# A decoder layer on one core: a later start for the down products' splits and loads, another order in the attention, outputs in steps

## The chip, the cores and the metric

The kernel runs on one NeuronCore of a Trainium2 chip. The metric is the device time of one execution in microseconds; the time given for a kernel is the median of several executions. A profile is taken of one more execution. TensorE does the matrix products and transposes, VectorE, ScalarE and GpSimd (in the profile DVE, ACT and POOL) do the rest, and SyncE (SP) only starts transfers.

## The reference

One layer of a hybrid decoder over 1024 tokens of width 1024, in float32:

```
h = x
h = h + 0.5 * swiglu(rms_norm(h), ffn1_w_gu, ffn1_w_down)
h = h + hybrid_mixer(rms_norm(h), ...)     # sparse attention, 8 heads | gated recurrence, 4 heads
h = h + 0.5 * swiglu(rms_norm(h), ffn2_w_gu, ffn2_w_down)
out = rms_norm(h)

swiglu(x) = (silu(gate) * up) @ w_down,  gate, up = x @ w_gu   # hidden width 2752
```

The attention has three branches for each head, each with its own softmax: over compressed keys (63 of them), over all earlier tokens (with 16 blocks of 64 tokens and 16 of them selected, the selected branch sees every earlier block), and over a window of 512 tokens. Scores carry a linear bias by distance. The three outputs are summed with sigmoid gates.

## The kernel before

**Numbers in two parts.** Every large product is done with operands split into a high part rounded for the fast float32 mode and a low part, the rest. `split` (L174) makes the high part on ScalarE (L180) or GpSimd (L178) and the low part on VectorE (L182). A product is three matmuls: high x high, high x low, low x high (L186 to L188 in `mm3`, L731 to L733 in `down`). The operand that streams through TensorE is read in an interleaved order there: `il` takes elements 0, n/2, 1, n/2+1 and so on, and whoever reads the result takes `ev(b)`, which undoes it.

**The two FFNs.** Both halves of each FFN use Strassen's scheme with seven products for eight. The up products (`up_rest`, `up_strassen`, `up_last`) run over 22 blocks of 128 hidden columns. Their results, and sums of them, go to DRAM as `H[...]` (`hid_put`, L548 to L562). For the last two blocks these stores sit on ScalarE's queue: the very last things that the up products put into the queues of VectorE and ScalarE are a subtraction (L562) and the store of its result (L556). Sums of the down weights are made on the way (`down_sums`, L581).

The second half, `down` (L700), has seven stages n with eleven steps m each. Step (n, m) loads a tile of the hidden sums and one of the down weights (L739 to L747, 256 KB each, on SP's queue), splits both, and adds 12 matmuls to four banks. Loads can run six steps ahead, for there are six pairs of buffers. The split tiles have their own buffers, two steps' worth in a pool that is open during the up products already. After some stages the four banks are added to the residual tiles `h` (`add`, L712), either at once or, from copies, at steps (n+1, 3), (n+1, 5), (n+1, 7) and (n+1, 9), as `later` says. `after` holds further work for given steps: the loads of the eight residual tiles (512 KB each, L1513 and L1811, eight steps from (0, 1) to (1, 4)), and in the first FFN the norm and the first weights of the mixer.

**What sets the order.** The program is written as one sequence. Tile, the layer below, puts the instructions of each engine in an order of its own at compile time, by the sequence and by when it expects operands to be ready, and an engine then takes its queue strictly in that order. So an instruction whose operands come early can be placed far ahead of its place in the program. `issue_after(i)` forbids that: what is traced under it stands behind `i` on the engine of `i`. `late()` (L143) does so for the last instruction traced so far on each of ScalarE, GpSimd, VectorE and SP.

**The attention.** For each of eight blocks of 128 queries (qb) and two groups of four heads (g), `att_soft` (L1216) does one head: score products (`prod`, L1239 and L1240), the bias and the row minimum in one VectorE instruction (`red`, L1245), exponentials with row sums on ScalarE (L1282), the reciprocal of the three sums on VectorE (L1285 for the first two heads together, L1288 for the others), and a scaling by reciprocal and gate on GpSimd (L1294). `att_pv` (L1299) then takes the four heads of a unit together: for each block of keys four transposes into a bank (L1325, two such banks), a copy to a high part on ScalarE (L1327), a low part on VectorE (L1328), and two value products (`pv`, L1316), which run two blocks behind. It is a generator that is advanced between the heads of the next unit.

**The end.** `finish` (L1817) is called for each token tile once per half of its columns. After the second it makes the final norm: a square sum, a power on GpSimd (`rsqrt`, L200), the scaled halves on VectorE (L1835) and ScalarE (L1843), and two stores of 256 KB.

Of the kernel before, what the change touches and what calls it, by code (L numbers as in the profile page):

```python
# [94 lines left out]
class Net:  # L95
# [15 lines left out]
    def consts(self, ctx):  # L111
        tc, nc = self.tc, self.nc
        c = self.cp = ctx.enter_context(tc.tile_pool(name="const", bufs=1))
        it = c.tile([128, D], F32, name="iota", tag="gb")[:, :128]
        nc.gpsimd.iota(it, pattern=[[1, 128]], base=0, channel_multiplier=-1,
                       allow_small_or_imprecise_dtypes=True)
        self.ident = c.tile([128, 128], F32, name="ident")
        self.mhalf = c.tile([128, 16], F32, name="mhalf")
        nc.gpsimd.memset(self.mhalf[:], -0.5)
        nc.vector.tensor_scalar(self.ident[:], it, 0.0, None, op0=OP.is_equal)  # L120

    def load_gain(self, ap):
# [16 lines left out]
        self.turn = 1 - self.turn  # L139
        return self.bank("ba"[self.turn])  # L140

    @contextmanager
    def late(self, pe=False):  # L143

        last = {}
        for i in self.nc.cur_bb.bb.instructions:
            last[i.engine] = i
        E = mybir.EngineType
        with ExitStack() as c:
            for e in (E.Activation, E.Pool, E.DVE, E.SP) + pe * (E.PE,):  # L150
                if e in last:
                    c.enter_context(self.tc.issue_after(last[e]))
            yield
# [547 lines left out]
    def down(self, pool, pool2, name, H, h, scale, final, after=(), wide=None, tail=0):  # L701
# [17 lines left out]
            return [nat(t[:]) for t in out]  # L719

        stages = (("A11", "B11"), ("A12", "B21"), ("S2", "T2"), ("S3", "T3"), ("A22", "T4"), ("S1", "T1"), ("S4", "B22"))
        later, behind = {}, None
        for n, (an, bn) in enumerate(stages):
            if n in (0, 2, 5):
                bs = [self.bank("b" if n == 2 else "a") for _ in range(4)]
# [9 lines left out]
            for m in range(11):  # L735
                i = n * 11 + m
                p, nb = (pool, 8) if i % 6 < 4 else (pool2, 4)
                raw, hr = (p.tile([128, 512], F32, name=self.nm("dr"), tag="dr", bufs=nb) for _ in range(2))
                nc.sync.dma_start(out=hr[:], in_=H[an][m])  # L739
                if bn in H:  # L740
                    nc.sync.dma_start(out=raw[:], in_=H[bn][m])
                else:
                    j, c = 2 * m + (bn != "B11"), 512 * (bn == "B22")
                    k = min(128, FF - j * 128)
                    if k < 128:
                        nc.gpsimd.memset(raw[k:], 0.0)
                    nc.sync.dma_start(out=raw[:k], in_=w_down[j * 128:j * 128 + k, c:c + 512])  # L747
                if wide is None and n < 6 and i % 5 > 1:
                    t2 = [self.xp.tile([128, 2, 512], F32R, name=self.nm("dw"), tag="xT", bufs=16) for _ in range(2)]
                    hh, hl, dh, dl = (t[:, k, :] for t in t2 for k in range(2))  # L750
                else:
                    p, nb = (pool2, 12) if wide and i % 5 > 1 else (pool, 8)
                    hh, hl, dh, dl = (p.tile([128, 512], F32R, name=self.nm("dw"), tag="dw", bufs=nb)[:] for _ in range(4))
                with self.tc.issue_after(behind) if behind and m > 1 else nullcontext():
                    self.split(hh, hl, hr[:], "act")
                self.split(dh, dl, raw[:])
                if n == 6 and m >= 11 - tail:
                    left.append((m, hh, hl, dh, dl))
# [456 lines left out]
    def att_soft(self, p, g, qb, hh):  # L1215
# [18 lines left out]
        wc = (qb + 1 - lo) * 128  # L1234
        cmp = P2[:, wc:wc + 64]

        def prod(ka, kl):
            b = self.bank()[:, :ka.shape[1]]
            mm(b, qa[:, qc], ka, start=True, stop=False)  # L1239
            mm(b, qa[:, qc], kl, start=False, stop=True)  # L1240
            return b

        def red(b, dst, tab, br, j):
            out = st[:, br:br + 1] if j == 0 else st[:, 9 + br:10 + br]
            nc.vector.tensor_tensor_reduce(out=dst, in0=b, in1=tab, op0=OP.add, op1=OP.min, scale=-slope,  # L1245
                                           scalar=3.0e38 if j == 0 else st[:, br:br + 1], accum_out=out)
            return out
# [3 lines left out]
        for br, s in ((2, 1), (1, 0)):  # L1251
            k0 = 0 if s == 0 else lo
            j = 0
            for half in range(2):
# [4 lines left out]
                c = (a % 4) * 128 + (0 if s else 576 - 64 * half)  # L1259
                pre = 64 if s == 0 and half == 0 and qb < 3 else 0  # L1260
                post = 64 if s == 1 and half == 0 and qb > 4 else 0
                b = prod(self.KA[g, half][:, c - pre:c + w + post], self.KL[g, half][:, c - pre:c + w + post])
                if pre:
                    bc = b[:, :64]
                if post:
# [3 lines left out]
                else:  # L1269
                    dst = P2[:, (a - lo) * 128:(e - lo) * 128]  # L1270
                    tab = self.dwin[:, 512 + (a - qb) * 128:512 + (e - qb) * 128]
                m = red(b[:, pre:pre + w], dst, tab, br, j)
                j += 1
            mx.append((br, m))
        if bc is None:
# [4 lines left out]
        def rest():  # L1280
# [1 line left out]
                nc.scalar.activation(out=rng[br], in_=rng[br], func=AF.Exp, scale=-1.0, bias=m,  # L1282
                                     accum_out=st[:, 6 + br:7 + br])
            if hh == 1:
                nc.vector.reciprocal(out=both[:, :, 6:9], in_=both[:, :, 6:9])  # L1285
                scaled(h - 1, both[:, 0, :], *before)
            elif hh:
                nc.vector.reciprocal(out=st[:, 6:9], in_=st[:, 6:9])  # L1288
            if hh:
                scaled(h, st, rng)  # L1290

# [8 lines left out]
    def att_pv(self, p, g, qb, Ps, raw, M):  # L1300
# [18 lines left out]
        for n, (i, c, w, v) in enumerate(blocks):  # L1319
# [8 lines left out]
            nc.vector.tensor_tensor(out=l[:w], in0=b[:w], in1=h[:w].bitcast(F32), op=OP.subtract)  # L1328
            th.append(h)
            tl.append(l)  # L1330
            if n > 1:
                pv(n - 2)
        pv(last - 1)
        pv(last)
        yield
        tmp = p.tile([128, 4, 128], F32, name=self.nm("ot"), tag="ph", bufs=4)[0:64]
        nc.scalar.activation(out=tmp.rearrange("p h (a b) -> p h a b", a=2), in_=ev(O[64:128], 64), func=AF.Copy)
        qc = slice((qb % 4) * 128, (qb % 4) * 128 + 128)
# [26 lines left out]
def body(ctx, tc, ins, out):  # L1365
# [146 lines left out]
        with net.late():  # L1512
            nc.sync.dma_start(out=h[tt][:], in_=x[tt * 128:(tt + 1) * 128, :])  # L1513

    for i, tt in enumerate((4, 5, 6, 7, 0, 1, 2, 3)):
        after[(0, 2 * i + 1) if i < 5 else (1, 2 * i - 10)] = lambda tt=tt: load(tt)

    def final(tt, c):
        net.square(np_, h[tt][:, c * 512:c * 512 + 512], sq[tt // 4][:, c, tt % 4:tt % 4 + 1])
# [283 lines left out]
    np_ = pool(ctx, "n3", "right")  # L1803
    net.load_gain(ins["final_norm"][None, :])
    h = [hp.tile([128, D], F32, name=f"k{tt}") for tt in range(NT)]
    sq = [np_.tile([128, 2], F32, name=f"sk{tt}") for tt in range(NT)]
    after, pend = {}, []

    def reload(tt):
        with net.late():  # L1810
            nc.sync.dma_start(out=h[tt][:], in_=spilled(tt))  # L1811

    for i, tt in enumerate((4, 5, 6, 7, 0, 1, 2, 3)):
        after[(0, 2 * i + 1) if i < 5 else (1, 2 * i - 10)] = lambda tt=tt: reload(tt)

    def finish(tt, c):
        k = slice(c * 512, c * 512 + 512)  # L1817
# [10 lines left out]
        y = np_.tile([128, D], F32, name=net.nm("y"), tag="y", bufs=4)  # L1828

        def store(i):  # L1830
            k = slice(i * 512, i * 512 + 512)
            (nc.sync if 4 <= tt < 7 or tt == 7 and i else nc.scalar).dma_start(out=out[0, tt * 128:(tt + 1) * 128, k], in_=y[:, k])

        def second():
            nc.vector.scalar_tensor_tensor(out=y[:, k], in0=hv, scalar=r, in1=net.gb[:, k], op0=OP.mult, op1=OP.mult)  # L1835
            store(1)

        r = net.rsqrt(np_, sq[tt][:, 0:1], 1, 1, "rs", sq[tt][:, 1:2])
        if 4 <= tt < 7:
# [4 lines left out]
        store(0)  # L1844

    net.down(f2, f2b, "ffn2", H, h, lambda tt: 0.5, finish, after, True, 5)
    cd.close()
# [18 lines left out]
```

## Time and profile before

| | us |
|---|---|
| median of 3 runs | 1904.49 (1901.87 to 1904.88) |
| the profiled execution | 1908.84 |
| its span, first to last instruction | 1907.1 |
| TensorE busy | 1876.7 (98%) |
| VectorE busy | 1348.6 (71%) |
| ScalarE busy | 787.2 (41%) |
| GpSimd busy | 524.4 (27%) |
| start of the down products, first FFN | 422.83 |
| start of the down products, second FFN | 1698.07 |
| last matmul starts | 1899.68 |

A matmul of 128x512 is shown with 0.38 us, but the next starts 0.215 us after it: matmuls are pipelined and their ends are modelled. TensorE's busy share says little; the distance from one start to the next, or the number of matmuls in a stretch, says whether it is held up. In a row of a timeline the first number is the start, the second the duration, and what stands in brackets is the idle time before it and what ended it. In a row of stretches each engine has its busy time and its number of instructions, and then come the granted share of TensorE's clock, the share of the DMA engines and GB/s. In a row of waits stand the sum, the number and the longest.

### The profile page before, as it was taken

How to read it: one execution, taken by the hardware profiler on the slowest of the kernel's cores; microseconds unless marked ns; L12 is line 12 of the kernel's file. 1: busy time of each engine (PE TensorE's matmuls, PEld its weight loads, DVE VectorE, ACT ScalarE, POOL GpSimd, SP SyncE). 2: the span in 40 equal slices, each digit the busy share in tenths (PEclk: the TensorE clock that was granted, in tenths of full speed). 3: DMA queues.
4: the chain of work that ended last, by engine and by line, in shares of the span. 5: the costliest groups of instructions: out<-in, count | busy, mean ns of one | idle time of the engine just before them, and what ended most of it. 6: DMA issues, size and time to landing. Idle time of an engine off the chain costs nothing.

```text
span 1907.1 us, 31154 instructions
## 1 busy us (share of the span) xinstructions
PE 1876.7 (98%) x11054; PEld 1622.4 (85%) x11054; DVE 1348.6 (71%) x2596; ACT 787.2 (41%) x1665; POOL 524.4 (27%) x634
## 2 busy tenths in 40 slices
PE   9999999999999999999999999999999999999998
PEld 6888888888888888889887788888888888888886
DVE  5988778658775545777278888836867777558676
ACT  5533333322323412333389776646333333323233
POOL 2133233324342001111156444311222222123222
PEclk9999999999999999999999999999999999999999
DMA  5346666438675132443321022462456676157664
GB/s 199 103 136 220 226 213 232 138 116 287 220 260 164 70 105 95 140 136 134 133 67 46 15 79 74 151 234 87 157 180 220 217 231 213 63 187 263 210 213 149
DMA packets 161787, 304.30 MB, mean 160 GB/s; under 512 B 17600, under 2 KB 47328, under 8 KB 161632
## 3 DMA queue, kind: packets, MB, share of 16 engines
q1 hardware_dynamic: 152096, 285.79, 45.4%
q10 hardware_dynamic: 9536, 16.53, 2.5%
q8 instruction: 87, 1.43, 0.3%
q14 instruction: 68, 0.56, 0.1%
HBM read 213.65 MB, written 88.60 MB: 158 GB/s over the span
## 4 chain that ended last, share of the span: by engine, by line
PE 84%; DVE 7%; ACT 3%; issue 2%; DMA 1%; POOL 1%; SPq 0%; POOLq 0%; DVEq 0%; ACTq 0%
PE b L186 17%; PE b L187 17%; PE b L188 17%; PE b L733 6%; PE b L731 6%; PE b L732 6%; PE b L1325 3%; PE b L1316 2%; PE b L1240 1%; PE b L1239 1%; ACT P L1282 1%; ACT ph L1327 1%; PE b L925 1%; PE b L796 1%; PE b L797 1%
## 5 line engine op out<-in xcount | busy, mean ns | idle before, releaser
L186 PE MATMUL b<-xT,wp 128*128 128x512 f32 x1196 | 455.4, 381 | 4.4 <-DVE pd L687 4.1
L187 PE MATMUL b<-xT,wp 128*128 128x512 f32 x1196 | 454.5, 380 | 1.5 <-DVE xT L425 1.3
L188 PE MATMUL b<-xT,wp 128*128 128x512 f32 x1196 | 453.8, 380 | 0.0
L182 DVE TENSOR_TENSOR dw<-dr,dw 128x512 fp32r<-128x512 f32 x308 | 231.5, 798 | 68.6 <-ACT dw L180 47.6
L186 PEld LDWEIGHTS b<-xT,wp 128*128 128x128 f32 x1196 | 226.6, 189 | 41.3 <-DVE pd L687 5.3
L187 PEld LDWEIGHTS b<-xT,wp 128*128 128x128 f32 x1196 | 226.5, 189 | 35.2 <-DVE xT L425 3.6
L188 PEld LDWEIGHTS b<-xT,wp 128*128 128x128 f32 x1196 | 226.4, 189 | 32.5
L733 PE MATMUL b<-dw,dw 128*128 128x512 f32 x616 | 235.1, 382 | 2.7 <-DVE dw L182 2.7
L731 PE MATMUL b<-dw,dw 128*128 128x512 f32 x616 | 235.2, 382 | 1.3 <-DVE dw L182 1.3
L732 PE MATMUL b<-dw,dw 128*128 128x512 f32 x616 | 234.5, 381 | 0.0
L178 POOL TENSOR_SCALAR dw<-dr 128x512 fp32r<-128x512 f32 x154 | 127.8, 837 | 254.8 <-PE b L733 130.6
L180 ACT ACTIVATE wp<-ws 128x512 fp32r<-128x512 f32 x148 | 92.9, 629 | 233.3 <-PE b L187 225.5
L180 ACT ACTIVATE dw<-dr 128x512 fp32r<-128x512 f32 x154 | 92.2, 625 | 198.7 <-PE b L731 88.0
L1294 POOL TENSOR_SCALAR P<-P,sm,gate 128x64 f32<-128x64 f32 (+8 forms) x192 | 125.7, 673 | 168.4 <-DVE sm L1285 99.1
L182 DVE TENSOR_TENSOR wp<-ws,wp 128x512 fp32r<-128x512 f32 x148 | 113.4, 768 | 30.7 <-ACT wp L180 30.5
L733 PEld LDWEIGHTS b<-dw,dw 128*128 128x128 f32 x616 | 117.1, 190 | 20.5 <-DVE dw L182 3.8
L731 PEld LDWEIGHTS b<-dw,dw 128*128 128x128 f32 x616 | 117.2, 190 | 18.8 <-issue 1.4
L732 PEld LDWEIGHTS b<-dw,dw 128*128 128x128 f32 x616 | 117.2, 190 | 16.8
L180 ACT ACTIVATE wp<-wr 128x512 fp32r<-128x512 f32 x115 | 71.9, 626 | 142.0 <-PE b L187 119.7
L1282 ACT ACTIVATE P<-P,sm 128x64 f32<-128x64 f32 (+8 forms) x192 | 114.7, 600 | 28.5 <-DVE sm L1245 27.5
L186 PE MATMUL b<-xT,wh 128*128 128x512 f32 x320 | 125.8, 394 | 0.0
L521 POOL TENSOR_TENSOR ws<-wr 128x512 f32<-128x512 f32 x37 | 51.6, 1396 | 263.9 <-DVE wp L182 215.4
(308 smaller groups left out, 3554.9 us busy)
## 6 DMA issues: line engine op xcount, KB each, us to landing
dr<-hs SPq DMA_DIRECT2D x242, 256.0 KB, 4.0
wr<-in_ffn_w_gu_dram SPq DMA_DIRECT2D x82, 512.0 KB, 4.2
hs<-hk SPq DMA_DIRECT2D x140, 256.0 KB, 3.9
hs<-wd SPq DMA_DIRECT2D x88, 256.0 KB, 3.1
wd<-in_ffn_w_down_dram SPq DMA_DIRECT2D x84, 256.0 KB, 3.5
dr<-in_ffn_w_down_dram SPq DMA_DIRECT2D x62, 256.0 KB, 4.2
wq<-wo SPq DMA_DIRECT2D x40, 256.0 KB, 2.9
wo<-wo SPq DMA_DIRECT2D x16, 512.0 KB, 2.6
```

What stands on the lines that cost most here:

```text
L178: nc.gpsimd.tensor_scalar(out=hi, in0=src, scalar1=1.0, scalar2=1.0, op0=OP.mult, op1=OP.mult)
L180: nc.scalar.activation(out=hi, in_=src, func=AF.Copy)
L182: eng.tensor_tensor(out=lo, in0=src, in1=hi.bitcast(F32), op=OP.subtract)
L186: mm(ps, wh, xh, start=first, stop=False, skip_group_check=skip)
L187: mm(ps, wh, xl, start=False, stop=False, skip_group_check=skip)
L188: mm(ps, wl, xh, start=False, stop=last, skip_group_check=skip)
L731: mm(bs[t][:], hl[:, c], dh, start=first, stop=False, skip_group_check=True)
L732: mm(bs[t][:], hh[:, c], dh, start=False, stop=False, skip_group_check=True)
L733: mm(bs[t][:], hh[:, c], dl, start=False, stop=last, skip_group_check=True)
L1282: nc.scalar.activation(out=rng[br], in_=rng[br], func=AF.Exp, scale=-1.0, bias=m, accum_out=st[:, 6 + br:7 + br])
L1294: nc.gpsimd.tensor_scalar(out=rng[br], in0=rng[br], scalar1=st[:, 6 + br:7 + br], scalar2=self.gate[:, qb, h * 3 + br:h * 3 + br + 1], op0 ...
L1325: nc.tensor.transpose(b[:w, hh * 128:hh * 128 + 128], Ps[hh][i][:, c:c + w], self.ident[:])
```

## The change

- `down` of both FFNs: the splits of steps m=1 to 10 of stage 0 stand behind the last instruction that each engine had when `down` was called. Those of m=0 stay free.
- The residual loads move from after steps (0, 1), (0, 3), (0, 5), (0, 7), (0, 9), (1, 0), (1, 2), (1, 4) for tiles 4 to 7 and 0 to 3 to (0, 5), (0, 7), (0, 9), (0, 10), (1, 1), (1, 2), (1, 4), (1, 5) for tiles 4, 0, 5, 1, 6, 2, 7, 3.
- Attention: score products whose bank holds no compressed part (no `pre`, no `post`) read the keys interleaved, and `red` undoes it. The sums are inverted by a power of -1 on GpSimd. Value products are issued in pairs after every second block, and the last two or three after the generator's last stop, so behind the next head's scores.
- The end: tiles 0 to 3 are no longer scaled in `finish`. One power serves all four, and steps (6, 3) to (6, 7) scale and store one tile each, on ScalarE's queue.

```
-        nc.gpsimd.memset(self.mhalf[:], -0.5)
+        nc.gpsimd.memset(self.mhalf[:, :8], -0.5)
+        self.mone = self.mhalf[:, 8:14]
+        nc.gpsimd.memset(self.mhalf[:, 8:], -1.0)
...
-    def late(self, pe=False):
+    def late(self, pe=False, last=None):
+        last = last or self.lasts()
...
-        later, behind = {}, None
+        later, behind, entry = {}, None, self.lasts()
...
-                with self.tc.issue_after(behind) if behind and m > 1 else nullcontext():
-                    self.split(hh, hl, hr[:], "act")
-                self.split(dh, dl, raw[:])
+                with self.late(last=entry) if n == 0 and m else nullcontext():
+                    with self.tc.issue_after(behind) if behind and m > 1 else nullcontext():
+                        self.split(hh, hl, hr[:], "act")
+                    self.split(dh, dl, raw[:])
...
+            if turn:
+                ka, kl = il(ka), il(kl)
             mm(b, qa[:, qc], ka, start=True, stop=False)
...
+            if turn:
+                dst, b, tab = nat(dst), ev(b), nat(tab)
             nc.vector.tensor_tensor_reduce(out=dst, in0=b, in1=tab, op0=OP.add, op1=OP.min, scale=-slope,
...
+                turn = not pre and not post
...
-                nc.vector.reciprocal(out=both[:, :, 6:9], in_=both[:, :, 6:9])
+                nc.gpsimd.tensor_tensor(out=both[:, :, 6:9], in0=both[:, :, 6:9], in1=self.mone.rearrange("p (a b) -> p a b", a=2), op=OP.pow)
...
-                nc.vector.reciprocal(out=st[:, 6:9], in_=st[:, 6:9])
+                nc.gpsimd.tensor_tensor(out=st[:, 6:9], in0=st[:, 6:9], in1=self.mone[:, :3], op=OP.pow)
...
-            if n > 1:
+            if n > 2 and n % 2:
+                pv(n - 3)
                 pv(n - 2)
-        pv(last - 1)
-        pv(last)
         yield
+        for n in range((last - 1) // 2 * 2, last + 1):
+            pv(n)
...
-    for i, tt in enumerate((4, 5, 6, 7, 0, 1, 2, 3)):
-        after[(0, 2 * i + 1) if i < 5 else (1, 2 * i - 10)] = lambda tt=tt: load(tt)
+    for g, tt in zip((5, 7, 9, 10, 12, 13, 15, 16), (4, 0, 5, 1, 6, 2, 7, 3)):
+        after[g // 11, g % 11] = lambda tt=tt: load(tt)
...
+    def early(tt):
+        with net.late():
+            if tt == 0:
+                Z["r"] = net.rsqrt(np_, sq4[:, 0, :], 4, 1, "rs4", sq4[:, 1, :])
+            if tt:
+                store(tt - 1, Z["y"], 1, nc.scalar)
+            if tt < 4:
+                r = Z["r"][:, tt:tt + 1]
+                y = Z["y"] = np_.tile([128, D], F32, name=net.nm("y"), tag="y", bufs=4)
+                nc.vector.scalar_tensor_tensor(out=y[:, 512:], in0=h[tt][:, 512:], scalar=r, in1=net.gb[:, 512:], op0=OP.mult, op1=OP.mult)
+                nc.scalar.activation(out=y[:, :512], in_=h[tt][:, :512], func=AF.Copy, scale=r)
+                store(tt, y, 0, nc.scalar)
+
+    for i in range(5):
+        after[6, 3 + i] = lambda tt=i: early(tt)
```

More of the change, by code (lines that the diff above doesn't have):

```diff
@@ L140, in bank2, with lasts @@
         return self.bank("ba"[self.turn])
-    @contextmanager
-    def late(self, pe=False):
+    def lasts(self):
         last = {}
@@ L147, in late @@
             last[i.engine] = i
+        return last
+    @contextmanager
+    def late(self, pe=False, last=None):
+        last = last or self.lasts()
         E = mybir.EngineType
@@ L1235, in att_soft, with prod @@
         cmp = P2[:, wc:wc + 64]
-        def prod(ka, kl):
+        def prod(ka, kl, turn=False):
             b = self.bank()[:, :ka.shape[1]]
+            if turn:
+                ka, kl = il(ka), il(kl)
             mm(b, qa[:, qc], ka, start=True, stop=False)
@@ L1241, in prod, with red @@
             return b
-        def red(b, dst, tab, br, j):
+        def red(b, dst, tab, br, j, turn=False):
             out = st[:, br:br + 1] if j == 0 else st[:, 9 + br:10 + br]
+            if turn:
+                dst, b, tab = nat(dst), ev(b), nat(tab)
             nc.vector.tensor_tensor_reduce(out=dst, in0=b, in1=tab, op0=OP.add, op1=OP.min, scale=-slope,
@@ L1261, in att_soft @@
                 post = 64 if s == 1 and half == 0 and qb > 4 else 0
-                b = prod(self.KA[g, half][:, c - pre:c + w + post], self.KL[g, half][:, c - pre:c + w + post])
+                turn = not pre and not post
+                b = prod(self.KA[g, half][:, c - pre:c + w + post], self.KL[g, half][:, c - pre:c + w + post], turn)
                 if pre:
@@ L1271, in att_soft @@
                     tab = self.dwin[:, 512 + (a - qb) * 128:512 + (e - qb) * 128]
-                m = red(b[:, pre:pre + w], dst, tab, br, j)
+                m = red(b[:, pre:pre + w], dst, tab, br, j, turn)
                 j += 1
@@ L1805, in body @@
     h = [hp.tile([128, D], F32, name=f"k{tt}") for tt in range(NT)]
-    sq = [np_.tile([128, 2], F32, name=f"sk{tt}") for tt in range(NT)]
-    after, pend = {}, []
+    sq4 = np_.tile([128, 2, 4], F32, name="sk")
+    sq = [sq4[:, :, tt] if tt < 4 else np_.tile([128, 2], F32, name=f"sk{tt}")[:] for tt in range(NT)]
+    after, pend, Z = {}, [], {}
     def reload(tt):
@@ L1811, in reload @@
             nc.sync.dma_start(out=h[tt][:], in_=spilled(tt))
-    for i, tt in enumerate((4, 5, 6, 7, 0, 1, 2, 3)):
-        after[(0, 2 * i + 1) if i < 5 else (1, 2 * i - 10)] = lambda tt=tt: reload(tt)
+    for g, tt in zip((5, 7, 9, 10, 12, 13, 15, 16), (4, 0, 5, 1, 6, 2, 7, 3)):
+        after[g // 11, g % 11] = lambda tt=tt: reload(tt)
     def finish(tt, c):
@@ L1827, in finish @@
             return
[L1828 to L1832, printed above, removed]
+        if tt < 4:
+            return
         def second():
             nc.vector.scalar_tensor_tensor(out=y[:, k], in0=hv, scalar=r, in1=net.gb[:, k], op0=OP.mult, op1=OP.mult)
-            store(1)
+            store(tt, y, 1, nc.sync)
+        y = np_.tile([128, D], F32, name=net.nm("y"), tag="y", bufs=4)
         r = net.rsqrt(np_, sq[tt][:, 0:1], 1, 1, "rs", sq[tt][:, 1:2])
-        if 4 <= tt < 7:
+        if tt < 7:
             pend.append(second)
@@ L1843, in finish, with store @@
         nc.scalar.activation(out=y[:, :512], in_=h[tt][:, :512], func=AF.Copy, scale=r)
-        store(0)
+        store(tt, y, 0, nc.sync if tt < 7 else nc.scalar)
+    def store(tt, y, i, queue):
+        k = slice(i * 512, i * 512 + 512)
+        queue.dma_start(out=out[0, tt * 128:(tt + 1) * 128, k], in_=y[:, k])
+    def early(tt):
[4 more added lines that the diff above has]
+                store(tt - 1, Z["y"], 1, nc.scalar)
+            if tt < 4:
+                r = Z["r"][:, tt:tt + 1]
[5 more added lines that the diff above has]
+        after[6, 3 + i] = lambda tt=i: early(tt)
     net.down(f2, f2b, "ffn2", H, h, lambda tt: 0.5, finish, after, True, 5)
```

## The prediction

> **What bounds the kernel now.** I read the page first, then stretches of the span, then the instructions around the few places where TensorE waits.
>
> ```profile
> span 1907.1 us, 31154 instructions
> PE 1876.7 (98%) x11054; PEld 1622.4 (85%) x11054; DVE 1348.6 (71%) x2596; ACT 787.2 (41%) x1665; POOL 524.4 (27%) x634
> ...
> 336.60:340.00 3.40, 3.40 (x10) 2.68 (x9) 2.02 (x3) 0.82 (x2) 2.66 (x3) 0.50 0.72 207
> 490.20:497.00 6.80, 6.13 (x14) 4.87 (x15) 4.86 (x10) 3.63 (x9) 1.56 (x3) 0.50 0.89 284
> 1700.00:1800.00 100.00, 100.00 (x465) 87.56 (x464) 79.56 (x110) 32.25 (x57) 35.61 (x40) 1.00 0.78 265
> ```
>
> TensorE is busy for 98%. The stretches give its pace: 465 matmuls in 100 us, 0.215 us each, when nothing is late. So only places below that pace can give time back, and a new wait of TensorE costs its full length. In two stretches the granted clock is 0.50: 10 and 14 matmuls where 15.8 and 31.6 would fit.
>
> **Change 1: early splits of the down products are queued later.** The splits of step m=1 of stage 0 now run long before TensorE needs them, inside the up products. There they do harm (GpSimd, VectorE, TensorE; then the same place of the second FFN):
>
> ```profile
> 331.77 0.62 POOL L178 TENSOR_SCALAR dw<-dr 128x512 fp32r<-128x512 f32 x1 [5.55 <-DMA dr<-in_ffn_w_down_dram]
> 332.42 0.69 DVE L182 TENSOR_TENSOR dw<-dr,dw 128x512 fp32r<-128x512 f32 x1 [0.84 <-POOL dw L178]
> 333.13 0.38 PE L188 MATMUL b<-xT,wp 128*128 128x512 f32 x1
> 335.57 0.48 PE L186 MATMUL b<-xT,wp 128*128 128x512 f32 x1 [2.06 <-DVE pd L687]
> ...
> 1588.76 0.62 POOL L178 TENSOR_SCALAR dw<-dr 128x512 fp32r<-128x512 f32 x1 [3.42 <-DMA dr<-in_ffn_w_down_dram]
> 1593.24 0.38 PE L188 MATMUL b<-xT,wp 128*128 128x512 f32 x1
> 1594.36 0.48 PE L186 MATMUL b<-xT,wp 128*128 128x512 f32 x1 [0.75 <-DVE pd L687]
> ```
>
> GpSimd holds its queue 5.55 us for a load; VectorE waits behind it; TensorE starts its next matmul 2.44 us after the last, 2.2 too late, and 3.4 us at half clock follow, which do the work of 1.7. With 0.1 for the exposed weight load: 4.1 us. At 1593 it is 1.12 - 0.215 = 0.9, with the weight load 1.0. After the change only m=0 is split early, so I take both back whole: -4.1 (0 if another load is waited for there) and -1.0 (0).
>
> The price lies at the start of the down products. Every split of m>=1 must follow the last instruction of the up products on its engine: on ScalarE that is the fourth store of the last hidden sums, which waits for VectorE's last subtraction.
>
> ```profile
> 416.02 2.90 DVE L182 TENSOR_TENSOR dw<-dr,dw 128x512 fp32r<-128x512 f32 x4
> 422.83 0.38 PE L731 MATMUL b<-dw,dw 128*128 128x512 f32 x1
> 428.97 0.69 DVE L562 TENSOR_TENSOR hk<-hk,hk 128x512 f32<-128x512 f32 x1 [1.99 <-DMA hs<-hk]
> 427.02 3.00 ACTq L556 DMA_DIRECT2D hs<-hk  x4
> 430.12 2.19 ACT L180 ACTIVATE dw<-dr 128x512 fp32r<-128x512 f32 x4 [3.85 <-DMA hs<-hk]
> ...
> 1698.07 0.38 PE L731 MATMUL b<-dw,dw 128*128 128x512 f32 x1
> 1700.31 0.69 DVE L182 TENSOR_TENSOR dw<-dr,dw 128x512 fp32r<-128x512 f32 x1
> 1701.67 1.92 ACTq L556 DMA_DIRECT2D hs<-hk  x4
> 1703.64 1.15 ACT L180 ACTIVATE dw<-dr 128x512 fp32r<-128x512 f32 x2 [3.23 <-DVE hk L562]
> ```
>
> Today splits of m=1 to 3 are done before (at 332 and at 416), and cover this chain: TensorE is full from 422.83 on. After the change m=0 alone covers it: 12 matmuls, 2.6 us, to 425.4. The ScalarE split of m=1 can start at 430.1, takes 0.6, its VectorE part 0.7: TensorE goes on at 431.4, a stall of 6.0. Without the wait of 1.99 on the store (the change moves residual loads of 512 KB out of this stretch) the chain is subtraction 427.0 to 427.7, stores to 428.5, split and rest 1.4: 429.9, a stall of 4.5. I take 5.0, nearer that end. Second FFN: 1698.07 + 2.6 = 1700.7; the split at 1703.64 + 1.3 gives 1705.0, a stall of 4.3; the split at 1700.31 then no longer stands in that chain on VectorE, which leaves 3.6. I take 3.9. After gaps of 2.4 and 2.9 us the clock halved for 3.4 and 6.8 us, so I add one such stretch to each, 1.7 (none to 3.4). Sum of this price: 5.0 + 3.9 + 3.4 = +12.3, between 4.5 + 3.6 = +8.1 and 6.0 + 4.3 + 6.8 = +17.1.
>
> [...]
>
> What a later TensorE meets: in the first FFN VectorE falls behind in stage 2.
>
> ```profile
> 456.00:490.00 34.00, 32.40 (x150) 27.75 (x148) 30.71 (x43) 7.64 (x15) 17.48 (x23) 1.00 0.74 236
> 488.02 0.38 PE L732 MATMUL b<-dw,dw 128*128 128x512 f32 x1
> 490.87 0.79 PE L733 MATMUL b<-dw,dw 128*128 128x512 f32 x1 [2.47 <-DVE dw L182]
> ```
>
> Here the gap is 2.85, of which 2.6 is lost, the matmul after it takes 0.4 more than its 0.38, and half clock over 6.8 us costs up to 3.4; I count 2.7, for 13 slow matmuls. After the change TensorE comes 6.7 later (5.0 + 1.7), and VectorE has six more splits to do by then (6 x 0.68 = 4.1): 2.6 us of relief against 3.0 of wait. I take 0.4 left and no half clock: -5.3 (0 to -5.7).
>
> **Change 2: residual loads.** The eight loads of 512 KB stay on SP's queue in both FFNs, but go after steps 5, 7, 9, 10, 12, 13, 15 and 16, where they were after 1 to 15, and in the order in which the additions of steps 14, 16, 18 and 20 take them. SP runs some six steps ahead, so none is late. What they free is in the chain above; nothing more is counted.
>
> **Change 3: the attention.** All products of this stage, what they wait for, and GpSimd's rows:
>
> ```profile
> L1239 PE MATMUL b<-ka,qa 128*128 128x512 f32 x72 | 29.8, 413 | 0.4 <-DVE sm L1245 0.4
> L1240 PE MATMUL b<-kl,qa 128*128 128x512 f32 x72 | 28.4, 395 | 0.0
> L733 PE MATMUL b<-dw,dw 128*128 128x512 f32 x155 | 58.7, 379 | 0.0
> L1316 PE MATMUL b<-ph,vhl 128*128 128x512 f32 x132 | 57.5, 435 | 3.7 <-ACT ph L1327 3.5
> PEld b L1325 <- DVE pt L1328: 14.2, 42, 0.8
> PEld b L1316 <- ACT ph L1327: 14.0, 37, 1.2
> L1288 DVE RECIPROCAL sm<-sm 128x3 f32<-128x3 f32 x32 | 5.6, 175 | 6.7 <-ACT P L1282 6.1
> L200 POOL TENSOR_TENSOR hr<-hr,mhalf 128x8 f32<-128x8 f32 x4 | 6.6, 1649 | 0.3
> L200 POOL TENSOR_TENSOR rs<-rs,mhalf 128x1 f32<-128x1 f32 x8 | 5.2, 657 | 18.7 <-DVE rs L199 18.7
> 1000.56 2.18 POOL P L1294 x5
> ...
> 1006.42 1.66 POOL P L1294 x3
> ```
>
> Score products without a compressed part now read the keys in the interleaved order of the other products. Those take 379 ns, these 413 and 395: 72 x 50 ns = 3.6 us at most. Waits are in these means too: -3.0 (0 to -3.6; shorter ones nothing). VectorE reads such a bank in both orders already, so I add nothing there.
>
> [...]
>
> Value products go in pairs, two blocks behind, and the last two or three after the next head's scores. That gives ScalarE's copies 0.4 us more (two products), about the mean wait (14.0/37); the waits of the transposes on VectorE stay, as their distance doesn't grow. Weight-load waits are partly covered: -3 (+2 to -9).
>
> Sums inverted on GpSimd: VectorE loses 48 short operations and their waits, 5.6 + 6.7 us in the row that holds 32 of them; a quarter of that on TensorE's path is -3 (0 to -10). GpSimd's power takes 657 ns for one column and 1649 for eight: 0.94 for three, 1.37 for six, 16 x 1.37 + 32 x 0.94 = 52 us in a stage where it is mostly idle. But early it is not: from 1000.56 to 1008.1 the chain runs through it, and a unit there would wait 1.37 + 2 x 0.94 = 3.2 us more. Three such units make 9.6; projections fill part: +3 (0 to +9.6).
>
> **Change 4: outputs in steps.** The first four output tiles are scaled behind the splits of steps 3 to 7 of the last stage, and one power replaces four.
>
> ```profile
> 1880.76:1889.80 9.04, 7.49 (x33) 5.54 (x32) 8.96 (x12) 2.79 (x5) 3.97 (x4) 1.00 0.05 20
> ```
>
> VectorE is full and TensorE does 33 matmuls where 42 fit: 1.9 lost. I take -1.5 (0 to -1.9). The end behind the last matmul is the same.
>
> **Sum.** 12.3 - 4.1 - 1.0 - 5.3 - 3.0 - 3 - 3 + 3 - 1.5 = -5.6 us. The profiled execution took 1908.84 us (span 1907.1 and 1.7 around it), which gives 1903.2; it lies 4.35 above the median of the runs, 1904.49, where the forecast is 1899.
>
> **Rivals.** A, slower: the stalls at the two starts take their upper prices, 17.1, from the point where m=1's split starts later than 2 us after m=0's products, and the wait at 488 stays because VectorE has as much more to do. 17.1 - 5.1 - 1.5 and the attention's -6 make +4.5: 1909. For it: VectorE at 30.7 of 34 us; against: the loads moved away from the first start.
> B, more gain: VectorE's freed time counts in full and the starts cost 8.1: 8.1 - 4.1 - 1.0 - 5.7 - 1.5, and in the attention -3.6 for the reading order and -7 for the rest, make -15: 1890. For it: two waits of 14 us in the attention.
> C, GpSimd becomes the bound of the first units, +9.6 for +3: 1905.5. For it: its rows on the chain; against: it is idle afterwards.
> D, the turned products are slowed by their reading order, as far as the 512-wide value products (435) lie above 404, 31 ns x 144 = +4.5 for -3: 1906.5. The interleaved 379 ns speak against it. [...]
>
> **Chances.** Forecast 0.33, A 0.30, B 0.21, C 0.13, D 0.03. A difference under 0.2% (3.8 us) is no change that can be told. The forecast, 3 us to either side, gives 0.23 faster and 0.10 same; A 0.21 slower, 0.08 same, 0.01 faster; B all faster; C 0.02, 0.07, 0.04; D 0.02 same, 0.01 slower. Sums: 0.47, 0.27, 0.26. The range reaches to both outer cases: 1888 to 1911; the forecast's own is 1896 to 1902.
>
> **What would show it.** No waiting split on GpSimd near 330 and 1588 and no gap of TensorE there; a gap of 4 to 6 us some 2.6 us after the first down product, then 0.50 of the clock; no 0.50 near 490; score products at 380 ns; a power before the scalings, and units near 1000 longer by up to 3 us. It is wrong if the start of the down products has no gap, or if splits of m=1 are early still.

## The result, and the profile after

The changed kernel is slower: 1922.97 us, the median of 5 runs (1921.03 to 1923.83), against 1904.49 before. The ratio is 1.0097, with a 95% interval of 1.0083 to 1.0112: 16 to 21 us. The forecast was 1899, with 1888 to 1911 around it. The profiled execution after took 1921.37 us, its span is 1919.6.

Where it went is seen in the distances between the first TensorE instructions of the stages (us; the second row ends at the last group of three down matmuls; the last row runs to the last matmul, and 7.4 follow in both kernels):

| stage | before | after | difference |
|---|---|---|---|
| start to down products, first FFN | 421.6 | 417.4 | -4.2 |
| down products, first FFN | 207.4 | 211.7 | +4.3 |
| mixer before the attention | 318.5 | 317.8 | -0.7 |
| attention | 303.1 | 313.4 | +10.3 |
| to the down products of the second FFN | 446.2 | 445.1 | -1.1 |
| down products, second FFN | 201.6 | 205.6 | +4.0 |

The two FFNs did nearly what was worked out for them; the attention did the opposite.

First the places in the FFNs. Stretches of the span of after (busy time of each engine and its instructions, then TensorE's granted clock):

```profile
333.00:337.00 4.00, 4.00 (x20) 3.50 (x19) 2.88 (x4) 1.55 (x3) 3.18 (x3) 1.00 0.78 256
1585.00:1600.00 15.00, 15.00 (x71) 13.12 (x71) 13.87 (x20) 5.79 (x10) 3.35 (x4) 1.00 0.64 205
1882.00:1912.00 30.00, 30.00 (x141) 26.27 (x140) 20.91 (x33) 13.33 (x28) 9.26 (x13) 1.00 0.41 146
...
424.40:431.20 6.80, 4.28 (x9) 3.02 (x10) 5.81 (x9) 3.34 (x6) 2.52 (x4) 0.50 0.77 247
```

At 0.215 us each, 4 us hold 18.6 matmuls, 15 us 69.8 and 30 us 139.5: the gaps at 333, at 1593 and in the last stage are gone. The last row is the price, 9 matmuls where 31.6 fit; the first 2.2 us of it are still the end of a wait. TensorE's and ScalarE's instructions around it (start, duration, and in brackets the idle time before):

```profile
420.97 0.38 PE L740 MATMUL b<-dw,dw 128*128 128x512 f32 x1
426.59 0.76 PE L738 MATMUL b<-dw,dw 128*128 128x512 f32 x1 [5.24 <-DVE dw L189]
...
1708.93 0.38 PE L740 MATMUL b<-dw,dw 128*128 128x512 f32 x1
1713.68 0.45 PE L738 MATMUL b<-dw,dw 128*128 128x512 f32 x1 [4.37 <-DVE dw L189]
```

```profile
421.47 0.63 ACT L551 ACTIVATE hk<-hk 64x512 f32<-64x512 f32 x1 [3.12 <-DVE hk L549]
422.85 1.83 ACTq L563 DMA_DIRECT2D hs<-hk  x4
424.73 2.71 ACT L187 ACTIVATE dw<-dr 128x512 fp32r<-128x512 f32 x5 [2.63 <-DMA hs<-hk]
```

The 12 matmuls of m=0 end their starts at 420.97. ScalarE's split of m=1 (L187) begins at 424.73, right behind the fourth store of the hidden sums (422.85 + 1.83), and TensorE goes on at 426.59: 5.4 us lost. In the second FFN it is 4.75 from start to start, 4.5 lost. In the first FFN the half clock lasts 6.8 us from 424.4 on, so 4.6 of them lie behind the wait; in the second 3.4 us follow, from 1714.7. Against 0.2155 us for each matmul TensorE loses 8.1 us around the first start and 6.4 around the second.

The gap of VectorE's making in stage 2 of the first FFN is still there, 2.14 from start to start and so 1.92 lost, but at full clock:

```profile
491.69 0.38 PE L739 MATMUL b<-dw,dw 128*128 128x512 f32 x1
493.83 0.48 PE L740 MATMUL b<-dw,dw 128*128 128x512 f32 x1 [1.76 <-DVE dw L189]
```

```profile
490.46 2.71 DVE L719 SCALAR_TENSOR_TENSOR h<-b,hr,h 128x512 f32<-128x512 f32 x4
```

Second the attention. Some of its groups and waits, after:

```profile
L1301 POOL TENSOR_TENSOR sm<-sm,mhalf 128x3 f32<-128x3 f32 x32 | 28.6, 893 | 16.7 <-ACT P L1295 16.6
L1298 POOL TENSOR_TENSOR sm<-sm,mhalf 128x6 f32<-128x6 f32 x16 | 21.3, 1332 | 110.2 <-ACT P L1295 91.1 <-DVE sm L1257 8.6 <-PE b L1250 7.3
L1249 PE MATMUL b<-ka,qa 128*128 128x512 f32 x72 | 28.7, 398 | 0.2 <-DVE sm L1257 0.2
L1250 PE MATMUL b<-kl,qa 128*128 128x512 f32 x72 | 27.5, 381 | 0.0
```

```profile
PEld b L1338 <- POOL P L1307: 8.9, 7, 2.5
PE b L1338 <- POOL P L1307: 7.5, 5, 2.3
PEld b L1329 <- ACT ph L1340: 8.3, 17, 1.1
```

The first of these rows in the kernel before:

```profile
PEld b L1325 <- POOL P L1294: 1.0, 3, 0.4
```

The power takes 893 and 1332 ns, close to the 0.94 and 1.37 us worked out. Waits of the value products on ScalarE's copies fell from 14.0 (37 of them) to 8.3 (17). What grew is the wait of the transposes for GpSimd's scalings: 8.9 us (L1338 for L1307), where it was 1.0 (L1325 for L1294). One stretch of 100 us holds most of the loss; before, then after:

```profile
980.00:1080.00 100.00, 95.11 (x552) 77.01 (x552) 92.03 (x307) 87.11 (x248) 61.64 (x101) 1.00 0.12 34
```

```profile
980.00:1080.00 100.00, 86.35 (x482) 72.13 (x481) 80.23 (x244) 78.74 (x225) 78.92 (x115) 0.95 0.10 33
```

TensorE, VectorE and ScalarE all do less in it; only GpSimd (the fifth pair of numbers) does more, 78.9% for 61.6%. The granted clock is 0.95 for 1.00: TensorE, which now waits, also meets three stretches of 3.4 us at half clock, from 987.6, 1014.9 and 1076.4.

### The profile page after: what moved, and what is told of

Same layout as the page of the kernel before. It is cut to its first block, busy times and chain, and to the rows that moved or that the text cites. A ratio compares the mean times of both kernels' runs of the same rounds, so it can differ in the third digit from the quotient of the medians.

```text
span 1919.6 us, 31168 instructions
## 1 busy us (share of the span) xinstructions
PE 1873.7 (98%) x11054; PEld 1626.8 (85%) x11054; DVE 1345.7 (70%) x2545; ACT 789.2 (41%) x1665; POOL 570.7 (30%) x680
## 5 line engine op out<-in xcount | busy, mean ns | idle before, releaser
L189 DVE TENSOR_TENSOR dw<-dr,dw 128x512 fp32r<-128x512 f32 x308 | 230.5, 798 | 66.8 <-ACT dw L187 53.9
L185 POOL TENSOR_SCALAR dw<-dr 128x512 fp32r<-128x512 f32 x154 | 123.9, 812 | 259.1 <-PE b L740 142.6
L187 ACT ACTIVATE wp<-ws 128x512 fp32r<-128x512 f32 x148 | 93.0, 630 | 233.9 <-PE b L194 226.3
L187 ACT ACTIVATE dw<-dr 128x512 fp32r<-128x512 f32 x154 | 92.3, 626 | 199.9 <-PE b L738 105.7
L187 ACT ACTIVATE wp<-wr 128x512 fp32r<-128x512 f32 x115 | 72.0, 627 | 141.5 <-PE b L194 111.2
L1307 POOL TENSOR_SCALAR P<-P,sm,gate 128x64 f32<-128x64 f32 (+8 forms) x192 | 126.3, 674 | 4.9
L1295 ACT ACTIVATE P<-P,sm 128x64 f32<-128x64 f32 (+7 forms) x192 | 114.9, 601 | 26.0 <-DVE sm L1257 25.3
```

Source lines behind the costliest of these rows:

```text
L185: nc.gpsimd.tensor_scalar(out=hi, in0=src, scalar1=1.0, scalar2=1.0, op0=OP.mult, op1=OP.mult)
L187: nc.scalar.activation(out=hi, in_=src, func=AF.Copy)
L189: eng.tensor_tensor(out=lo, in0=src, in1=hi.bitcast(F32), op=OP.subtract)
L1307: nc.gpsimd.tensor_scalar(out=rng[br], in0=rng[br], scalar1=st[:, 6 + br:7 + br], scalar2=self.gate[:, qb, h * 3 + br:h * 3 + br + 1], op0 ...
```

## The experiments

Where nothing else is said, an experiment is the kernel before with one edit, and its ratio is to runs of the kernel before on the same chip.

### 1. Is it the power? Two parts of the attention alone

The power alone (pow_only):

```
-                nc.vector.reciprocal(out=both[:, :, 6:9], in_=both[:, :, 6:9])
+                nc.gpsimd.tensor_tensor(out=both[:, :, 6:9], in0=both[:, :, 6:9], in1=self.mone.rearrange("p (a b) -> p a b", a=2), op=OP.pow)
...
-                nc.vector.reciprocal(out=st[:, 6:9], in_=st[:, 6:9])
+                nc.gpsimd.tensor_tensor(out=st[:, 6:9], in0=st[:, 6:9], in1=self.mone[:, :3], op=OP.pow)
```

> The kernel before with one edit: the sums are inverted by the power on GpSimd. Theory 1 (the power is in the chain of the first units): the stretch from the first score product to the last value product grows from 303 us by 8 to 13 us, all of it in units with fewer than 12 key blocks, and the whole kernel by about as much, to 1912 to 1918. Theory 2 (the new order of the value products makes the loss): the stretch changes by less than 3 us and the kernel stays within 1900 to 1908.

Measured: 1917.51 (1916.02 to 1919.25), ratio 1.0067 [1.0050, 1.0084]. The attention takes 314.8 us, 11.7 more than before; no other stage differs by more than 1.6. This edit alone makes more than half of the whole loss. The transposes wait 8.4 us for the scalings. Its first units:

```profile
980.00:1080.00 100.00, 87.05 (x484) 70.69 (x484) 80.64 (x245) 77.60 (x221) 78.15 (x115) 0.97 0.11 33
```

The order of the value products alone (pv_only):

```
-            if n > 1:
+            if n > 2 and n % 2:
+                pv(n - 3)
                 pv(n - 2)
-        pv(last - 1)
-        pv(last)
         yield
+        for n in range((last - 1) // 2 * 2, last + 1):
+            pv(n)
```

> The kernel before with one edit: value products in pairs, and the last ones behind the next head's scores. Theory 1 (the power makes the loss): the attention's 303 us shrink by 1 to 4 us, 1900 to 1904 in all. Theory 2 (the order makes it): they grow by 5 to 10 us, to 1909 to 1915, with waits of value products on VectorE of several us.

Measured: 1900.88, ratio 0.9983 [0.9974, 0.9992]; the attention takes 300.6, 2.5 less. The wait it was meant for is halved here too:

```profile
PEld b L1316 <- ACT ph L1327: 7.3, 17, 1.2
```

### 2. The start of the down products

The later splits alone (split_only):

```
+                with self.late(last=entry) if n == 0 and m else nullcontext():
```

> The kernel before with one edit: the splits of m=1 to 10 of stage 0 stand behind the up products. Theory 1: gaps of 5 to 6 us and 4 to 5 us some 2.6 us after the first down product of each FFN, each with a stretch at half clock, for no gap at 333 and at 1593 and a shorter one near 490. Sum: +5.5 +4.5 + 3 to 5 for the clock, -4.1 -1.0 -3 to -6: 2 to 7 us slower, 1907 to 1911. Rival (the gaps at the starts come from the moved loads or from the attention's shift): no gap there, 1898 to 1902.

Measured: 1913.99, ratio 1.0048 [1.0033, 1.0063]. That is 9.1 us more than the kernel before, where 2 to 7 were expected. The profiled executions, from which the terms were taken, lie 4.6 apart (1911.7 and 1907.1). TensorE's two gaps:

```profile
420.82 0.38 PE L738 MATMUL b<-dw,dw 128*128 128x512 f32 x1
427.00 0.76 PE L736 MATMUL b<-dw,dw 128*128 128x512 f32 x1 [5.81 <-DVE dw L187]
...
1698.75 0.38 PE L738 MATMUL b<-dw,dw 128*128 128x512 f32 x1
1703.61 0.46 PE L736 MATMUL b<-dw,dw 128*128 128x512 f32 x1 [4.49 <-DVE dw L187]
```

Without the moved loads 6.0 and 4.6 us are lost, with them 5.4 and 4.5: the loads shorten the first stall by 0.6, where the upper and the lower end of the forecast lay 1.5 apart.

The whole change with the reciprocals back on VectorE (no_pow):

> The changed kernel with the reciprocals back on VectorE, all else as changed. Theory 1: the attention comes back from 313 to 299 to 302 us, and the kernel from 1923 to 1908 to 1912. Theory 2: it stays above 308 us, and the kernel above 1917.

Measured: 1909.41, ratio 1.0023 [1.0013, 1.0032]; attention 299.7. Against the changed kernel's 1922.97 the power alone is worth 13.6 us, in the company of the other edits about as much as by itself. What is left is 4.5 us slower than before, although the attention is 3.4 us shorter than before here: that loss lies on the FFNs' side of the change.

Then the same kernel with the splits held less far back (mid_no_pow): the mark is taken ahead of the last block of the up products (`up_last`), so that splits may stand among that block's instructions, in front of its stores, but not earlier.

```
+        self.entry = self.lasts()
         self.up_last(pool, cpool, 21, raws[21], R, H)
...
-        later, behind, entry = {}, None, self.lasts()
+        later, behind, entry = {}, None, self.entry
```

> The changed kernel with reciprocals on VectorE (as in no_pow) and the splits of m=1 to 10 held back only to the last instruction before block 21 of the up products, not behind block 21 itself. Theory 1 (the gaps at the starts come from standing behind the last store of block 21): both gaps of 4.5 to 5.4 us and their stretches at half clock vanish, those at 333 and 1593 stay away; a wait near 490 of 1 to 3 us may come back. 1894 to 1900. Rival (the gaps come from splits that are late for another reason, as VectorE's load or the transfers): gaps of over 2 us remain after the first down products, 1903 to 1908.

Measured: 1895.43 (1895.26 to 1896.49), ratio 0.9955 [0.9940, 0.9970]: 14 us below the version above (13 by the two ratios), and faster than the kernel before. ScalarE's queue and TensorE's pace at the start:

```profile
412.82 1.66 ACT L185 ACTIVATE dw<-dr 128x512 fp32r<-128x512 f32 x3
...
422.40 0.63 ACT L549 ACTIVATE hk<-hk 64x512 f32<-64x512 f32 x1 [3.12 <-DVE hk L547]
422.94 0.61 ACT L185 ACTIVATE dw<-dr 128x512 fp32r<-128x512 f32 x1
423.78 4.13 ACTq L561 DMA_DIRECT2D hs<-hk  x4
428.01 2.71 ACT L185 ACTIVATE dw<-dr 128x512 fp32r<-128x512 f32 x5 [4.46 <-DVE hk L567]
```

```profile
418.00:431.00 13.00, 13.00 (x62) 11.37 (x62) 9.54 (x14) 4.49 (x8) 7.54 (x8) 1.00 0.99 371
```

Three splits run at 412.82 and one at 422.94, in front of the four stores; in the changed kernel ScalarE had none between 408 and 424.73. TensorE does 62 matmuls in 13 us at full clock (60.5 fit), and the gaps at 333 and 1593 are gone as well. So the stalls were the price of how far the splits were moved, not of moving them.

### 3. The gap at 488

In the kernel of mid_no_pow the gap lies at 484, and VectorE shows what stands in front of the split: four additions in a row (2.71 us), as at 490.46 in after. They are the four that close stage 1. They were put one by one behind steps 1, 3, 5 and 7 of stage 2 (mid_spread):

```
+                    if n == 1:
+                        later.setdefault((2, 1 + 2 * t), []).append(lambda a=(half, t, c, ev(bs[t][:])): add(*a))
+                        later.setdefault((2, 2 + 2 * t), []).append(lambda a=(half * 4 + t, c): final(*a))
+                        continue
                     add(half, t, c, ev(bs[t][:]))
```

> The version with the splits held at the last up block and reciprocals on VectorE (median 1895.43), with one more edit: the four additions that end stage 1 of the down products are no longer traced in a block at the end of the stage but one at a time, after steps 1, 3, 5 and 7 of stage 2, each square sum a step later. Theory (four additions of 2.71 us in a row hold VectorE in front of the split that TensorE waits for; VectorE is not behind by more than that): the gap of 2.64 us near 484 is gone, with the half clock behind it 1.7 us more: 1891 to 1893, down products to the attention 203 or less. Rival (VectorE carries a backlog from stage 1 that any later work meets): the gap moves to the next additions or splits in stage 2, 1895 to 1896, no change.

Measured: 1892.14 (1891.43 to 1892.61), ratio 0.9937 [0.9924, 0.9951], the fastest version of all. VectorE, and a stretch of 17 us in mid_no_pow and then in this kernel:

```profile
482.80 0.74 DVE L718 SCALAR_TENSOR_TENSOR h<-b,hr,h 128x512 f32<-128x512 f32 x1
483.46 0.53 DVE L187 TENSOR_TENSOR wl<-wr,wh 128x256 fp32r<-128x256 f32 x1
483.92 0.88 DVE L187 TENSOR_TENSOR dw<-dr,dw 128x512 fp32r<-128x512 f32 x1
484.72 0.74 DVE L718 SCALAR_TENSOR_TENSOR h<-b,hr,h 128x512 f32<-128x512 f32 x1
```

```profile
483.00:500.00 17.00, 14.53 (x61) 12.01 (x60) 14.36 (x22) 6.13 (x14) 7.52 (x10) 0.90 0.78 243
```

```profile
483.00:500.00 17.00, 16.49 (x77) 14.13 (x76) 15.39 (x24) 6.02 (x14) 7.93 (x11) 1.00 0.83 263
```

77 matmuls for 61, at full clock; 0.7 us are still lost. VectorE was hardly further behind than by these four instructions.

### 4. What of the power costs: early units, GpSimd's time, or the hand-over?

The power for query blocks 5 to 7 only, the reciprocal on VectorE for 0 to 4 (pow_late), at both places:

```
+                if qb > 4:
+                    nc.gpsimd.tensor_tensor(out=st[:, 6:9], in0=st[:, 6:9], in1=self.mone[:, :3], op=OP.pow)
+                else:
+                    nc.vector.reciprocal(out=st[:, 6:9], in_=st[:, 6:9])
```

> The kernel before with the power on GpSimd for query blocks 5 to 7 only; blocks 0 to 4 keep the reciprocal on VectorE. If the loss of pow_only sits in the early units alone, the attention takes 302 to 304 us as before and the kernel 1902 to 1907. If the power costs wherever it is used, the attention grows by 3 to 6 us. If VectorE's freed time counts once the chain is out of the way, it shrinks by 1 to 4 us.

Measured: 1904.14, ratio 0.9999 [0.9990, 1.0009]; attention 302.8. The six units of blocks 5 to 7 neither lose nor gain: GpSimd has room there (34% busy from 1086 to 1250 in the kernel before), and VectorE's freed time is worth nothing there. The loss is made in the first ten units. Starts of the first transposes, counted from those of the first unit: block 1, second group, 30.0 us before and 33.4 with the power alone; block 2, second group, 53.9 and 63.6; block 4, first group, 101.9 and 115.0. From there on it stays at 11 to 13.

To part GpSimd's time from the hand-over, the reciprocals stay on VectorE and GpSimd does the same power behind each of them as well, into a tile that nobody reads (dummy_pow), again at both places:

```
                 nc.vector.reciprocal(out=st[:, 6:9], in_=st[:, 6:9])
+                nc.gpsimd.tensor_tensor(out=self.spare[:, :3], in0=st[:, 6:9], in1=self.mone[:, :3], op=OP.pow)
```

> The kernel before, reciprocals on VectorE as they were, and behind each of the 48 the same power on GpSimd, whose result goes into a tile that nobody reads. It leaves nothing out; it adds 50 us of GpSimd time and no new hand-over. Theory (time in GpSimd's queue ahead of the scalings is the price): about what the power costs when it replaces the reciprocal, 1914 to 1919, attention 313 to 317. Rival (the price is that the power stands in VectorE's place, so the order of VectorE's queue or the hand-over from ScalarE to GpSimd is what counts): 1904 to 1908, attention 303 to 306.

Measured: 1914.66 (1913.48 to 1916.03), ratio 1.0054 [1.0036, 1.0072]; attention 313.7, 10.6 more than before, and much the same delays (block 4, first group, at 112.5). The transposes wait 10.2 us for the scalings. The useless powers and the stretch of the first units:

```profile
L1293 POOL TENSOR_TENSOR spare<-sm,mhalf 128x3 f32<-128x3 f32 x32 | 27.5, 858 | 18.2 <-DVE sm L1292 18.1
L1289 POOL TENSOR_TENSOR spare<-sm,mhalf 128x6 f32<-128x6 f32 x16 | 21.2, 1328 | 119.5 <-DVE sm L1288 111.4 <-DVE sm L1248 8.1
```

```profile
977.00:1077.00 100.00, 87.59 (x487) 70.38 (x486) 81.39 (x270) 78.44 (x223) 77.41 (x116) 0.97 0.11 33
```

The other engines' instructions are not slowed by the added work. VectorE's low parts in the first ten units, before and here:

```profile
L1328 DVE TENSOR_TENSOR pt<-b,ph 128x512 fp32r<-128x512 f32 x70 | 47.0, 687 | 7.8 <-ACT ph L1327 7.2
L1333 DVE TENSOR_TENSOR pt<-b,ph 128x512 fp32r<-128x512 f32 x70 | 47.1, 689 | 9.3 <-ACT ph L1332 8.8
```

ScalarE's copies take 590 ns before and 591 here. So nearly all of the price is time in GpSimd's queue ahead of the scalings, with the half clock that follows: two stretches of 3.4 us in the attention here and with the power alone, three in the changed kernel, none in the kernel before.

Does the reverse hold, so that GpSimd's time is also worth something when it is taken away? In mid_spread the scaling of the compressed part (64 columns) of blocks 0 to 4 was given to VectorE (mid_vec):

```
-                nc.gpsimd.tensor_scalar(out=rng[br], in0=rng[br], scalar1=st[:, 6 + br:7 + br],
+                (nc.vector if br == 0 and qb < 5 else nc.gpsimd).tensor_scalar(out=rng[br], in0=rng[br], scalar1=st[:, 6 + br:7 + br],
```

> The version with the splits held at the last up block, reciprocals on VectorE and the four additions spread (median 1892.14), with one more edit: in the first ten units of the attention (query blocks 0 to 4) the scaling of the compressed part, 64 columns, runs on VectorE in place of GpSimd: 40 instructions of 411 ns, 16 us, leave GpSimd, and come to VectorE, which is 92% busy there. Theory (GpSimd's time in these units is on the path, as 31 us of powers cost 11.7): at that rate 16 us less give up to 6 back: 1886 to 1890, attention 294 to 297. Rival (the path goes through GpSimd only when it is lengthened; VectorE and ScalarE bound the units as they are): no gain, 1892 to 1898, attention 299.5 to 305.

Measured: 1898.80, ratio to the kernel before 0.9979 [0.9970, 0.9988], where mid_spread had 0.9937: slower. The attention takes 307.7 us for 299.5 in the profiles; but the profiled execution is the slowest of eleven (1903.92), so the stage's 8 us are an upper end, and 6.8 us at half clock from 1066.5 on make up to 3.4 of them; 2.2 us more lie in its first FFN, which the edit doesn't touch.

```profile
L1310 DVE TENSOR_SCALAR P<-P,sm,gate 128x64 f32<-128x64 f32 x40 | 16.5, 428 | 0.3
```

```profile
973.00:1073.00 100.00, 92.41 (x517) 75.16 (x516) 95.41 (x323) 85.49 (x240) 47.91 (x68) 0.97 0.11 33
```

GpSimd fell to 48% from the 63% of mid_spread and nothing came of it; VectorE, at 95% for 93%, seems to set the pace. The 40 instructions take as long there as on GpSimd, 428 ns for the 411 of the kernel before. So the first units seem to have little room on either engine: GpSimd's time counts when it is lengthened, and shortening it this way gives nothing. Whether it would without the load on VectorE wasn't tried.

### 5. The small terms

The interleaved reading alone, `turn = not pre and not post` with what hangs on it (turn_only):

> The kernel before, with the one edit that score products without a compressed part read the keys interleaved, and the bias and minimum read the bank accordingly. Theory from the means of the rows (413 and 395 ns before, 398 and 381 with the whole change): 144 products shorter by about 15 ns, 2 us at most, of which 0.9 shows in the attention: 1903 to 1904.5. Rival (the forecast's value, 3 us back): 1901.5, attention 300. Rival (the order costs TensorE or VectorE something elsewhere): above 1905.

Measured: 1902.95, ratio 0.9997 [0.9988, 1.0007]; attention 302.2, 0.9 less.

```profile
L1241 PE MATMUL b<-ka,qa 128*128 128x512 f32 x72 | 28.7, 398 | 0.4 <-DVE sm L1249 0.4
L1242 PE MATMUL b<-kl,qa 128*128 128x512 f32 x72 | 27.3, 379 | 0.0
```

The products are 15 and 16 ns shorter, 144 x 15.5 = 2.2 us at most, and not all of it is on the path. The rows are shorter; the kernel's time can't be told from that of the kernel before.

The outputs in steps alone (`early`, with one power for four tiles; out_only):

> The kernel before with one edit: the first four output tiles are scaled in steps behind the splits of the last stage. The lost time of TensorE of 2.2 us in the last 15 us before its end goes to below 0.5: 1 to 2 us faster, 1902 to 1904. Rival (the transfers set that wait): no change of these gaps, 1904 to 1906.

Measured: 1901.10, ratio 0.9982 [0.9972, 0.9991]; the last stage's gaps are gone, its FFN's down products take 199.2 for 201.6.

```profile
1876.00:1893.00 17.00, 17.00 (x81) 14.88 (x80) 10.92 (x18) 6.49 (x13) 3.61 (x6) 1.00 0.26 96
```

The residual loads alone (loads_only):

> The kernel before with one edit: the residual loads of both FFNs later and in pairs. If VectorE's work sets the wait at 488, that gap stays at 2.3 to 2.9 us, and the kernel within 2 us of before. If the transfers set it, the gap shrinks below 1.5 us and the half clock after it goes: 2 to 6 us faster.

Measured: 1902.89, ratio 0.9993 [0.9984, 1.0002]: no change that can be told. The gap is still there, 2.66 us from start to start, with no half clock behind it in this profile, so it is VectorE's work and not the transfers that makes it:

```profile
484.99 0.38 PE L732 MATMUL b<-dw,dw 128*128 128x512 f32 x1
487.65 0.48 PE L733 MATMUL b<-dw,dw 128*128 128x512 f32 x1 [2.28 <-DVE dw L182]
```

## Why the prediction was wrong

The sum of the forecast against the two profiled executions (span 1907.1 to 1919.6):

| term | forecast | measured | by |
|---|---|---|---|
| stalls at the two starts | +8.9 | +9.9 | after: 5.4 and 4.5 |
| half clock and slow start behind them | +3.4 | +4.6 | 8.1 + 6.4 lost in all, less 9.9 |
| gap at 333 | -4.1 | -4.2 | stage before it |
| gap at 1593 | -1.0 | -1.1 | stage before it |
| gap at 488 | -5.3 | -3.9 | 6.0 lost there before, 2.1 after |
| outputs | -1.5 | -2.4 | rest of the last stage |
| mixer before the attention | 0 | -0.7 | difference of the stages |
| attention | -6 | +10.3 | difference of the stages |
| sum | -5.6 | +12.5 | |

The 18.1 us between the two sums are the attention, 16.3, and small differences of both signs.

**The step that failed: the power on GpSimd, "+3 (0 to +9.6)".** Its duration was right. The count was not: "three such units make 9.6; projections fill part", worked out from a chain through GpSimd near 1000. The power alone costs 11.7 in the attention, net of whatever VectorE gains by it, and the useless power 10.6, so the term lies outside its own bounds, and in the company of the other edits it is 313.4 - 299.7 = 13.7. Ten units come before block 5, each with 1.33 + 2 x 0.893 = 3.1 us of powers, 31 us; and for these TensorE loses 11 to 14, the half clock behind its new waits included. The delays are spread over the units: 3.5 us by the second group of block 1, 9.7 by that of block 2, 13.1 by the first of block 4. The row that could have warned of it is the stretch of 100 us: GpSimd 62% busy, and some seven units' powers, 22 us, to come into a chain that also has to wait for ScalarE. "A stage where it is mostly idle" was true of the mean alone. Rival C named this mechanism and place; its size and its chance, 0.13, were too small.

**VectorE's freed time, "-3 (0 to -10)", was nothing.** pow_late frees 18 of the 48 reciprocals where GpSimd costs nothing, and the attention stays at 302.8 for 303.1. In the early units it was not seen apart from the power, but there is no sign of it: pow_only, which frees VectorE, takes 1.1 us more in the attention than dummy_pow, which doesn't.

**The value products, -3: right.** 2.5 in the attention, 4.0 between the medians, with an interval of 1.5 to 5.

**The interleaved reading, -3: too large, and shown in the rows only.** The reading took 15 and 16 ns off, where 34 and 16 lay between these products and the interleaved ones of the FFNs (413 and 395 to 379), and 0.9 us off the stage. Rival D, slower for the same edit, fell: 398 and 379 ns lie below 413 and 395. Only the keys are read with a stride there, and the products write their bank in order in both kernels, so these rows compare the order of reading alone.

**The starts of the down products: right.** The chain over the fourth store, its place and length (5.0 and 3.9 forecast), were as worked out; the half clock lasted twice as long in the first FFN, but 2.2 us of it fell into the wait itself. The sum, 14.5, lies inside 8.1 to 17.1. Rival A, with 17.1, was about as far off on the other side, and its total was too low for the same reason as the forecast's.

**The gap at 488: right for a reason that doesn't hold.** The wait shrank by 0.7, from 2.64 to 1.92, not by 2.6 (by 1.4 in no_pow, whose code is the same up to there); the rest of the 3.9 is the half clock that followed in the profiled execution of before. VectorE was not in a backlog that a later TensorE lets it work off: the wait is four additions in a row, and mid_spread takes it away by spreading them. And the half clock isn't in every execution (below), so a gain counted from one execution that lay 4.35 us above the median was partly there already in the median. The medians differ by 18.5 and the spans by 12.5; between them lie this 4.35, and 1.6 by which the profiled execution of after lies under its own median.

**The outputs, -1.5: right in sign, somewhat small.** 2.4 in the last stage, with the whole change and alone; between the medians 3.2.

**The gap at 333, -4.1: right.** The terms named for it add to 4.0, and 4.0 are lost there in the kernel before.

The attention's terms measured one by one, 11.7 - 2.5 - 0.9, make 8.3 for the 10.3 seen together. The clock in the first units is 0.95 with the whole change and 0.97 with the power alone: one more stretch of 3.4 us at half clock, which is up to 1.7 of the other 2 us. Whether these are the same 2 us was not settled.

## What to carry to other kernels

An engine's mean load over a stage says nothing on what a new instruction costs there: take the load stretch by stretch, and where every unit of a loop goes through the engine, count the instruction once for each such unit, not once for each unit on the chain that the profile happens to show. That count is an upper bound: of 31 us here, 11 to 14 came. When a piece of work is forbidden to run too early, the mark can be put between the two harms: ahead of the last block, not behind its last store, made 13 to 14 us of difference here. A wait on a busy engine isn't always a backlog; look which instructions stand in front, for four short ones in a row can be spread.

## What the runs showed of the hardware

The half clock after a short gap comes in some executions and not in others. The same gap of 2.86 us from start to start is followed by 3.4 us at 0.50 in mid_no_pow and by none with the interleaved reading alone (below: the two gaps, then a stretch of the latter):

```profile
483.77 0.38 PE L738 MATMUL b<-dw,dw 128*128 128x512 f32 x1
486.62 0.80 PE L739 MATMUL b<-dw,dw 128*128 128x512 f32 x1 [2.47 <-DVE dw L187]
```

```profile
485.38 0.38 PE L732 MATMUL b<-dw,dw 128*128 128x512 f32 x1
488.24 0.48 PE L733 MATMUL b<-dw,dw 128*128 128x512 f32 x1 [2.48 <-DVE dw L182]
```

```profile
483.00:500.00 17.00, 14.52 (x66) 11.94 (x65) 14.59 (x22) 6.01 (x14) 8.25 (x11) 1.00 0.77 237
```

The first matmul behind the gap takes 0.80 us in the one and 0.48 in the other. Seven of the profiles have a gap of this length at this place: in four half clock follows (the kernel before, pow_only, mid_no_pow, out_only), in three it doesn't (pow_late, dummy_pow, turn_only). The time goes with it: of 19 executions of the kernel before on one chip, the five with a mean granted clock of 0.999 took 1902.5 to 1903.7 us, the one with 0.996 took 1908.6. In the kernel before, the stretches at half clock ahead of the last matmul last 3.4 us (from 336.6 on) and 6.8 (from 490.2); in the changed kernel 6.8 (from 424.4) and 3.4 (from 987.6, 1014.9, 1076.4 and 1714.7). What sets these lengths, and which executions meet half clock behind such a gap, was not shown. In mid_no_pow the gap of 2.86 us from start to start did harm: 61 matmuls in the 17 us around it, where 66 came with the interleaved reading alone. For a sum such a gap is better priced by its chance, four of seven here, than by the one execution at hand.
